# State-space layer: decay rows kept in DRAM in 4 copies, each read by 32 partitions, in place of 16 copies read by 8

## The chip, the core and the metric

The kernel runs on one core of one Trainium2 chip. The metric is the device time of one execution in microseconds; the time before is the median of 3 runs. A profiled execution of the same kernel gives the trace that all lines below come from; times in the trace count from the start of its span.

A core has a matmul engine (TensorE, PE in the profile, with its weight loads as PEld), a vector engine (VectorE, DVE), an engine for functions such as exp (ScalarE, ACT), a general engine (GpSimd, POOL) and an engine that here only issues DMA transfers (SyncE, SP). Sixteen DMA engines carry the transfers. Each engine runs its own instructions in a fixed order and waits on semaphores for the others. SBUF is the on-chip memory with 128 partitions, PSUM the accumulator of TensorE, DRAM the memory behind the DMA engines.

## The reference

The model is a trunk of two layers over 512 tokens of width 1024. Each layer is a feed-forward half step, a mixer and a second feed-forward half step, each with a layer norm. The mixer of the first layer is a bidirectional state-space layer with 32 heads of width 64, 4 groups of B and C, state size 128; that of the second layer is attention. What matters here, cut down:

```python
dt = softplus(dt_raw.reshape(b, t, 2, SSM_HEADS) + dt_bias)
A  = -exp(a_log)
# per direction, per head, in chunks:
a_cs         = cumsum(dt * A)
L            = exp(segsum(a))              # exp(a_cs[l] - a_cs[s]), masked to s <= l
CB           = einsum('bclgn,bcsgn->bgcls', Cc, Bc)
y_diag       = einsum('bgcls,bgjcls,bcsgjp->bclgjp', CB, L, Xc)
states       = einsum('bclgn,bgjcl,bclgjp->bcgjpn', Bc, exp(a_cs[-1] - a_cs), Xc)
y_off        = einsum('bclgn,bcgjpn,bgjcl->bclgjp', Cc, states, exp(a_cs))
y            = y_diag + y_off              # forward, and the same on the flipped sequence
y            = (y_f + y_b + X * d_skip) * silu(z)   # then a grouped RMS norm and a projection
```

So each head needs a decay matrix exp(a_cs[l] - a_cs[s] + log dt[s]) of tokens by tokens for each direction, and a row exp(a_cs[l]).

## The kernel before

Everything is kept transposed: features on the partitions, the 512 tokens along the free dimension. Weights come in units of 128 x 1024 floats (`load`, L99, one 512 KB transfer into one of four `raw` buffers), are split into a rounded high part (ScalarE, L123) and a low part (VectorE, L124), and each product is three matmuls (`mm3`, L166).

The function `ssm` (L589) is the state-space layer. `dt_proj` and `dt_chain` compute the cumulated decays with small matmuls and turn them so that heads lie on partitions and tokens along the free dimension: `rows` holds 32 heads of forward and 32 of backward decays, `rowe` the exponentials of them that go with the states. `dt_chain` ends with four transfers (L667) that write these rows to a DRAM tile `scr` (L602) of shape copies x 32 heads x 3 rows x 512 tokens. The write repeats each row once for every copy; its outer dimension is the 32 heads.

`ssd_head` (L757) is called for each of the 32 heads. It loads two rows of the head, spread over all 128 partitions, into the tile `rw` (L761, 512 KB, two buffers) and the third into `ch` (L763, 256 KB, three buffers), so that every partition (a source token s) holds the row over the destination tokens l. The source pattern is copies x (partitions per copy, step 0) x contiguous floats; rw reads 4 KB per partition, ch 2 KB. `ssd_head` then multiplies `ch` with C (VectorE, L764) and masks triangles of `rw` into `rw` and `dx` with GpSimd (L778).

`ssd_mats` (L783) builds for a head and a half (c = 0 or 1) of the tokens the matrix E: four exponentials on ScalarE (L786 to L789) with the source token's term as bias, a sum on GpSimd (L792) and a product with C·B on VectorE (L793). E has five buffers. `ssd_out` (L796) multiplies E, the states and `ch` into the PSUM tile `py`, whose pool tag is "mid" (L803); two heads share one `py`, so heads go in pairs, 16 pairs in all. After the second half of a pair VectorE adds the result into `xs` (L874).

The heads are dealt with in four groups of eight (`for g in range(NG)`). Between the steps of a group stand weight units as filler for TensorE: the next group's B, C and x projections, this group's z projections, and the output projection of the group before (`todo`, L863, L881). The layer ends with the norm of the last group and its output projection.

The order in which each engine runs its instructions is planned when the kernel is built, from the dependences, the order of the program text and estimated times; buffers of a pool are handed out in turn, and a transfer into a buffer waits until the last reader of its previous contents is done. All loads and the `scr` transfers are issued by SyncE in one queue.

Of the kernel before, what the change touches and what calls it, by code (L numbers as in the profile page):

```python
# [9 lines left out]
F32 = mybir.dt.float32  # L10
# [4 lines left out]
P = 128  # L15
T = 512
# [4 lines left out]
NA = 32  # L21
NE = 5
NG = 4
NST = 128
ALPHA = 4.0 ** 0.25
EPS = 1e-5
# [20 lines left out]
def hybrid_trunk(tc, xT, cb, par, cst, adaw, wgu, wdn0, wdn1, wdn2, wdt, win, wso, wqk, wv, wao, dist_in, dtp, lam_in, out):  # L47
    nc = tc.nc
# [13 lines left out]
    def big(dt=F32, name="big"):  # L62
        return ap.tile([P, T], dt, tag="a", name=name)

    def tmp(name="tmp"):
        return tp.tile([P, T], F32, tag="t", name=name)

    def acc(tag="acc"):
        return ps.tile([P, T], F32, tag=tag, name=tag, bufs=BANKS[tag])
# [519 lines left out]
    def ssm(n):  # L589
# [3 lines left out]
        dp = sc.enter_context(tc.tile_pool(name="dp", bufs=1, space=bass.MemoryType.DRAM))  # L593
# [5 lines left out]
        W = 256  # L599
        bias = ep.tile([P, 4, 64], F32, name="ssbias", bufs=1)  # L600
        dd = ep.tile([P, 4, 32], F32, name="dd", bufs=1)
        scr = dp.tile([16, 32, 3, T], F32, name="scr")  # L602

        def dt_proj():
            w = split(load(wdt, 512))
            pd = acc("mid")
            wk = [(w.hi[:, k * 64 : (k + 1) * 64], w.lo[:, k * 64 : (k + 1) * 64]) for k in range(KT)]
            proj(pd, wk, u, m=64, cols=HALVES)
            return pd

        def dt_chain(pd):
            dtT = tmp("dtT")
            nc.scalar.activation(dtT[:64], pd[:64], AF.Copy)
            pt = acc("ln")
            for i in range(4):
                nc.tensor.transpose(pt[:, i * 64 : (i + 1) * 64], dtT[:64, i * P : (i + 1) * P], ident[:64, :64])
            e1, e2, e3 = (ep.tile([P, T], F32, tag="E", name="E", bufs=NE) for _ in range(3))
            v, q, e, uu, lu = e1[:, :W], e1[:, W:], e2[:, :W], e2[:, W:], e3[:, :W]
            nc.vector.tensor_tensor(out=v, in0=pt[:, :W], in1=dtc[:, :W], op=ALU.add)
            nc.vector.scalar_tensor_tensor(out=q, in0=v, scalar=-1.0, in1=v, op0=ALU.mult, op1=ALU.max)  # L620
            nc.scalar.activation(e, q, AF.Exp, scale=-1.0)
            ea = e3[:, W:]
            nc.scalar.activation(ea, dtc[:, W:], AF.Exp)
            nc.vector.tensor_scalar(out=v, in0=v, scalar1=0.0, scalar2=None, op0=ALU.max)
            nc.vector.tensor_scalar(out=uu, in0=e, scalar1=1.0, scalar2=None, op0=ALU.add)
            nc.scalar.activation(lu, uu, AF.Ln)
            nc.vector.tensor_scalar(out=uu, in0=uu, scalar1=1.0, scalar2=None, op0=ALU.subtract)
            nc.vector.tensor_tensor(out=uu, in0=e, in1=uu, op=ALU.subtract)
            nc.vector.tensor_scalar(out=e, in0=e, scalar1=-0.5, scalar2=1.0, op0=ALU.mult, op1=ALU.add)
            nc.vector.tensor_tensor(out=uu, in0=uu, in1=e, op=ALU.mult)  # L630
            nc.vector.tensor_tensor(out=lu, in0=lu, in1=uu, op=ALU.add)
            nc.vector.tensor_tensor(out=v, in0=v, in1=lu, op=ALU.add)
            at = q
            nc.vector.scalar_tensor_tensor(out=at, in0=v, scalar=-1.0, in1=ea, op0=ALU.mult, op1=ALU.mult)
            nc.vector.tensor_scalar(out=v, in0=v, scalar1=1e-37, scalar2=None, op0=ALU.max)
            nc.scalar.activation(lu, v, AF.Ln)
            pcs = acc("ln")
            nones = tmp("nones")[:, :P]
            nc.gpsimd.memset(nones, -1.0)
            plan = {  # L640
                (0, 0): [(sgt, 0), (nones, 1)], (0, 1): [(sgt, 1)],
                (0, 2): [(sle, 2)], (0, 3): [(ones, 2), (sle, 3)],
                (1, 0): [(sge, 0), (ones, 1)], (1, 1): [(sge, 1)],
                (1, 2): [(slt, 2)], (1, 3): [(nones, 2), (slt, 3)],
            }
            for (dr, i), lst in plan.items():
                for k, (mk, j) in enumerate(lst):
                    nc.tensor.matmul(
                        pcs[:, i * 64 + dr * 32 : i * 64 + dr * 32 + 32], lhsT=mk,
                        rhs=at[:, j * 64 + dr * 32 : j * 64 + dr * 32 + 32],  # L650
                        start=k == 0, stop=k == len(lst) - 1,
                    )
            cs = tmp("cs")[:, :W]
            nc.scalar.activation(cs, pcs[:, :W], AF.Copy)
            nc.vector.tensor_tensor(out=bias.rearrange("p i h -> p (i h)"), in0=lu, in1=cs, op=ALU.subtract)
            pr = acc("ln")
            for i in range(4):
                nc.tensor.transpose(pr[:64, i * P : (i + 1) * P], cs[:, i * 64 : (i + 1) * 64], ident)
            rows = big(name="rows")
            nc.scalar.activation(rows[:64], pr[:64], AF.Copy)  # L660
            rowe = big(name="rowe")
            nc.scalar.activation(rowe[32:64, :W], pr[32:64, :W], AF.Exp)
            nc.scalar.activation(rowe[0:32, W:], pr[0:32, W:], AF.Exp)
            nc.scalar.activation(dd[:, 0:2, :], bias[:, 0:2, 0:32], AF.Exp)
            nc.scalar.activation(dd[:, 2:4, :], bias[:, 2:4, 32:64], AF.Exp)
            for j, a, b, src in ((0, 0, T, rows[0:32]), (1, 0, T, rows[32:64]), (2, 0, W, rowe[32:64]), (2, W, T, rowe[0:32])):
                nc.sync.dma_start(  # L667
                    scr[:, :, j, a:b].rearrange("r h x -> h r x"), src[:, a:b].unsqueeze(1).broadcast_to([32, 16, b - a])
                )

        last_in, last_exp = [None], [None]
# [24 lines left out]
        def units_bc(g, dst, cols=FULL, pre=None):  # L696
            def mk(e):
                return lambda: dst.append(conv(pre[e] if pre else split(load(win[g * 10 + e])), 16 + 4 * e + g, cols))
            return [mk(e) for e in range(2)]
# [57 lines left out]
        def ssd_head(h, Ct):  # L757

            src = scr[:, h].unsqueeze(1)
            rw = ep.tile([P, 2, T], F32, tag="rw", name="rw")  # L760
            nc.sync.dma_start(rw, src[:, :, 0:2].broadcast_to([16, 8, 2, T]))  # L761
            ch = ep.tile([P, T], F32, tag="ch", name="ch", bufs=3)
            nc.sync.dma_start(ch, src[:, :, 2].broadcast_to([16, 8, T]))  # L763
            nc.vector.tensor_tensor(out=ch, in0=ch, in1=Ct, op=ALU.mult)  # L764
            dx = ep.tile([P, 2, 2, P], F32, tag="dx", name="dx")
            f4 = rw[:, 0, :].rearrange("p (c o q) -> p c o q", c=2, o=2)
            b4 = rw[:, 1, :].rearrange("p (c o q) -> p c o q", c=2, o=2)
            for o, i_, fwd in (
                (f4[:, :, 0, :], f4[:, :, 0, :], True), (b4[:, :, 1, :], b4[:, :, 1, :], False),
            ):  # L770
                mask(o, i_, fwd)
            for o in range(2):
                mask(dx[:, :, o, :], (b4 if o == 0 else f4)[:, :, o, :], o == 1, inplace=False)
            return rw, ch, dx

        def mask(o, i_, fwd, inplace=True):
            sg = 1 if fwd else -1
            nc.gpsimd.affine_select(  # L778
                out=o, in_=i_, pattern=[[0, 2], [sg, P]], compare_op=ALU.is_ge,
                fill=-1.0e30, base=0, channel_multiplier=-sg,  # L780
            )
# [52 lines left out]
        def run(units):  # L834
            for f in units:
                f()

        pre = first_units(n)
        pd = dt_proj()
        bc, xs, zs = [], [], [[] for _ in range(NG)]  # L840
        run(units_bc(0, bc, cols=HALVES, pre=pre))
# [14 lines left out]

        for g in range(NG):
            xt, cbs, states, Ct = cur
            nbc, nxs = [], []
            first = units_z(g, zs[g])[len(zs[g]) :]  # L860
            if g < NG - 1:
                first = units_bc(g + 1, nbc) + units_x(g + 1, nxs) + first
            todo = first + ([lambda gg=g - 1: outp(gg)] * 4 if g > 0 else [])  # L863
            tot, done, batched = len(todo), 0, False
            for s in range(8):
# [13 lines left out]
                if s == 2 and norm is not None:  # L879
                    yrs[g - 1] = rest()  # L880
                while done < tot - (2 if g == NG - 1 else 0) and done < (s + 1) * tot // 8:  # L881
                    todo[done]()
                    done += 1
                if done >= len(first) and not batched and (s >= 6 or done == tot):
                    batched = True
                    silu(zs[g] + nbc + nxs)
                    if g < NG - 1:
                        cur = prepare(g + 1, nxs, nbc)
# [3 lines left out]
        run(todo[done:])  # L892
        for _ in down_units(n, yr, wide_units(wso[NG - 1]), True, 6):
            pass
# [168 lines left out]
    for d in range(KT):  # L1063
# [9 lines left out]
        for o in (hl[0], uf):  # L1073
            x = nc.scalar.activation(o, res[d], AF.Identity, bias=shift[0][:, d : d + 1], scale=onep[0][:, d : d + 1])
# [122 lines left out]
```

## Time and profile before

| | |
|---|---|
| median of 3 runs | 2179.48 us (2178.3 to 2181.34) |
| profiled execution, its own time | 2176.88 us |
| span of its trace | 2174.8 us |
| mean granted TensorE clock | 0.993 |
| busy share of the span: PE, PEld, DVE, ACT, POOL | 97%, 86%, 82%, 50%, 7% |
| DMA: bytes, mean rate | 301.18 MB, 138 GB/s |
| written to DRAM | 5.24 MB |
| first and last issue of an `rw` load | 429.0 us, 745.6 us |
| writes of `scr`: first and last issue | 416.9 us, 420.0 us |

How to read the lines. A row of a timeline has the start in us, the length in us, the engine, the line of the program, the operation, the tile written and the tiles read, their sizes, and a count; a bracket at the end gives idle time of the engine just before and what ended it. "SPq" rows are issues of transfers. A row of waits has who waited and for whom, us in all, times, and the longest. A row of a queue has packets, MB and the share of the time of all 16 DMA engines that the packets took. Shares of busy time are averages over stages that have different limits.

### The profile page before, as it was taken

What the parts mean: (1) busy time and instruction counts of PE and PEld (TensorE: products, weight loads), DVE (VectorE), ACT (ScalarE), POOL (GpSimd) and SP (SyncE); (2) the same over time, 40 slices, a digit from 0 to 9 for tenths busy, and PEclk for the clock granted to TensorE, in tenths of its full rate; (3) what the DMA queues carried; (4) which work ended last, traced back from release to release, by engine and by line L of the source; (5) the groups of instructions that cost most, each with busy time, mean ns of one, the idle gap of its engine ahead of it and who ended that gap; (6) DMA issues with size and microseconds to landing.
All of it is one profiled execution on the core that took longest, in us unless ns stands there. A gap on an engine that the chain in (4) does not pass through costs nothing.

```text
span 2174.8 us, 34198 instructions
## 1 busy us (share of the span) xinstructions
PE 2119.9 (97%) x13206; PEld 1859.7 (86%) x13206; DVE 1775.3 (82%) x3086; ACT 1092.4 (50%) x1828; POOL 154.2 (7%) x258
## 2 busy tenths in 40 slices
PE   7999999999999989999999999999999989999997
PEld 6889899866777778999999989899888869989897
DVE  6979899556766689989889998987877879858697
ACT  4424354767655546434356534343866637424353
POOL 0000000045232300000000000000111100000000
PEclk9999999999999999999999999999999989999999
DMA  9863644464535423646443273723322212323231
GB/s 324 302 212 121 219 138 149 123 183 137 158 123 155 121 68 126 214 144 198 159 132 105 97 261 96 254 94 111 98 80 79 76 59 78 127 69 117 84 110 39
DMA packets 90082, 301.18 MB, mean 138 GB/s; under 512 B 10048, under 2 KB 13504, under 8 KB 89920
## 3 DMA queue, kind: packets, MB, share of 16 engines
q1 hardware_dynamic: 88384, 294.81, 41.7%
q0 software_dynamic: 1536, 4.20, 0.9%
q8 instruction: 103, 1.69, 0.3%
q14 instruction: 59, 0.48, 0.1%
HBM read 289.53 MB, written 5.24 MB: 136 GB/s over the span
## 4 chain that ended last, share of the span: by engine, by line
PE 59%; DVE 3%; issue 2%; ACT 2%; POOL 1%; DMA 0%; POOLq 0%; ACTq 0%; DVEq 0%; SPq 0%
PE acc L166 47%; PE mid L166 9%; PE mid L965 1%; PE ln L166 1%; PE ln L987 0%; DVE resid L278 0%; DMA raw<-in_wgu 0%; DVE resid L320 0%; PE ln L253 0%; PE ln L302 0%; ACT p L975 0%; POOL E L792 0%; ACT wh L123 0%; PE ln L1004 0%; DVE p L968 0%
## 5 line engine op out<-in xcount | busy, mean ns | idle before, releaser
L166 PE MATMUL acc<-hi,wh 128*128 128x256 f32 (+1 forms) x1592 | 533.1, 336 | 9.2 <-DVE resid L372 7.1
L166 PE MATMUL acc<-hi,wl 128*128 128x256 f32 (+1 forms) x1592 | 532.6, 335 | 0.0
L166 PE MATMUL acc<-lo,wh 128*128 128x256 f32 (+1 forms) x1592 | 532.1, 335 | 0.1
L166 PE MATMUL acc<-uh,wh 128*128 128x256 f32 (+1 forms) x1160 | 391.2, 338 | 0.0
L166 PE MATMUL acc<-ul,wh 128*128 128x256 f32 (+1 forms) x1160 | 389.6, 336 | 0.0
L166 PE MATMUL acc<-uh,wl 128*128 128x256 f32 (+1 forms) x1160 | 388.9, 336 | 0.0
L123 ACT ACTIVATE wh<-raw 128x1024 fp32r<-128x1024 f32 (+1 forms) x210 | 212.8, 1021 | 277.5 <-PE acc L166 95.4
L166 PEld LDWEIGHTS acc<-hi,wh 128*128 128x128 f32 x1592 | 302.9, 190 | 45.5 <-DVE resid L372 6.6
L470 ACT ACTIVATE wh<-raw 128x1024 fp32r<-128x1024 f32 x198 | 209.1, 1059 | 259.4 <-DVE raw L480 129.1
L166 PEld LDWEIGHTS acc<-lo,wh 128*128 128x128 f32 x1592 | 302.9, 190 | 31.0 <-DVE lo L154 1.3
L166 PEld LDWEIGHTS acc<-hi,wl 128*128 128x128 f32 x1592 | 303.0, 190 | 30.3 <-issue 0.5
L124 DVE TENSOR_TENSOR wl<-raw,wh 128x1024 fp32r<-128x1024 f32 (+1 forms) x210 | 248.4, 1185 | 46.7 <-ACT wh L123 45.4
L471 DVE TENSOR_TENSOR wl<-raw,wh 128x1024 fp32r<-128x1024 f32 x198 | 240.8, 1219 | 38.9 <-ACT wh L470 38.1
L166 PEld LDWEIGHTS acc<-uh,wh 128*128 128x128 f32 x1160 | 219.0, 189 | 28.6 <-issue 6.2
L166 PEld LDWEIGHTS acc<-ul,wh 128*128 128x128 f32 x1160 | 219.3, 189 | 25.1 <-issue 3.2
L166 PEld LDWEIGHTS acc<-uh,wl 128*128 128x128 f32 x1160 | 219.2, 189 | 23.7 <-issue 2.4
L480 DVE TENSOR_TENSOR raw<-raw 128x512 f32<-128x512 f32 x264 | 181.3, 688 | 5.0
L184 DVE SCALAR_TENSOR_TENSOR raw<-raw,cond 128x1024 f32<-128x1024 f32 x144 | 174.1, 1218 | 9.9 <-DMA raw<-in_adaw 9.7
L372 DVE SCALAR_TENSOR_TENSOR resid<-acc,gv,resid 128x512 f32<-128x512 f32 (+1 forms) x166 | 109.4, 663 | 58.8 <-PE acc L166 58.4
L316 POOL TENSOR_TENSOR rr<-vr,mhalf 128x2 f32<-128x2 f32 x12 | 8.4, 698 | 1527.6 <-DVE vr L312 1527.6
L166 PE MATMUL mid<-uh,wh 128*128 128x256 f32 (+2 forms) x332 | 99.8, 302 | 0.0
L166 PE MATMUL mid<-uh,wl 128*128 128x256 f32 (+2 forms) x332 | 99.3, 299 | 0.0
(266 smaller groups left out, 3920.7 us busy)
## 6 DMA issues: line engine op xcount, KB each, us to landing
raw<-in_wgu SPq DMA_DIRECT2D x176, 512.0 KB, 4.2
raw<-in_adaw SPq DMA_DIRECT2D x144, 512.0 KB, 4.6
raw<-in_wdn SPq DMA_DIRECT2D x64, 448.0 KB, 4.0
raw<-in_win SPq DMA_DIRECT2D x40, 512.0 KB, 4.2
raw<-in_wdn SPq DMA_DIRECT2D x32, 512.0 KB, 4.4
rw<-scr SPq DMA_DIRECT2D x32, 512.0 KB, 5.5
ch<-scr SPq DMA_DIRECT2D x32, 256.0 KB, 3.6
raw<-in_wso SPq DMA_DIRECT2D x16, 512.0 KB, 3.5
```

The source lines that it names most:

```text
L123: nc.scalar.activation(hi[:, :n], raw, AF.Copy)
L124: nc.vector.tensor_tensor(out=lo[:, :n], in0=raw, in1=hi[:, :n].bitcast(F32), op=ALU.subtract)
L166: last = nc.tensor.matmul(o, lhsT=a, rhs=b, start=start and j == 0, stop=j == n - 1, skip_group_check=not start)
L184: nc.vector.scalar_tensor_tensor(out=raw, in0=raw, scalar=1.0, in1=cond, op0=ALU.mult, op1=ALU.mult, accum_out=mods[l][:, j : j + 1],)
L316: nc.gpsimd.tensor_tensor(out=r[:, :m], in0=vr[:, :m], in1=mhalf[:, :m], op=ALU.pow)
L372: nc.vector.scalar_tensor_tensor(out=res[d][:, a:b], in0=pd[:, a:b], scalar=gvec[n][:, d : d + 1], in1=res[d][:, a:b], op0=ALU.mult, op1=A ...
L470: nc.scalar.activation(x[0], r, AF.Copy)
L471: nc.vector.tensor_tensor(out=x[1], in0=r, in1=x[0].bitcast(F32), op=ALU.subtract)
L480: nc.vector.tensor_tensor(out=o, in0=x, in1=y, op=ALU.add)
L965: nc.tensor.matmul(ss[m], lhsT=q[:, c], rhs=qks[h, 1][m], start=j == 0, stop=j == 1)
```

## The change

The number of copies becomes a constant NREP = 4. The DRAM tile `scr` gets 4 copies instead of 16, the four writes repeat each row 4 times instead of 16, and each of the 64 loads of `rw` and `ch` reads 4 copies, each by 32 partitions, instead of 16 copies by 8. The number of transfers, the bytes each load brings into SBUF and all computation stay as they are.

```diff
+NREP = 4
...
-        scr = dp.tile([16, 32, 3, T], F32, name="scr")
+        scr = dp.tile([NREP, 32, 3, T], F32, name="scr")
...
                 nc.sync.dma_start(
-                    scr[:, :, j, a:b].rearrange("r h x -> h r x"), src[:, a:b].unsqueeze(1).broadcast_to([32, 16, b - a])
+                    scr[:, :, j, a:b].rearrange("r h x -> h r x"), src[:, a:b].unsqueeze(1).broadcast_to([32, NREP, b - a])
                 )
...
-            nc.sync.dma_start(rw, src[:, :, 0:2].broadcast_to([16, 8, 2, T]))
+            nc.sync.dma_start(rw, src[:, :, 0:2].broadcast_to([NREP, P // NREP, 2, T]))
             ch = ep.tile([P, T], F32, tag="ch", name="ch", bufs=3)
-            nc.sync.dma_start(ch, src[:, :, 2].broadcast_to([16, 8, T]))
+            nc.sync.dma_start(ch, src[:, :, 2].broadcast_to([NREP, P // NREP, T]))
```

## The prediction

> **What bounds the kernel now.** I read the page, then busy time by stretch of the state-space stage, then waits, then the order of time. The page:
>
> ```profile
> DMA packets 90082, 301.18 MB, mean 138 GB/s; under 512 B 10048, under 2 KB 13504, under 8 KB 89920
> q1 hardware_dynamic: 88384, 294.81, 41.7%
> ```
>
> The DMA engines are 42% used over the span, so they do not bound it as a whole. The 10,048 packets under 512 B are 628 transfers with 16 each: every transfer of this kernel was spread over all 16 engines. The heads of the stage run from about 429 to 771 us; busy time by stretch (PE, PEld, DVE, ACT, POOL; clock; DMA share):
>
> ```profile
> 429.00:530.00 101.00, 95.45 (x432) 64.63 (x432) 57.66 (x75) 67.86 (x146) 43.39 (x71) 0.98 0.64 172
> 720.00:771.00 51.00, 48.31 (x245) 35.15 (x243) 34.71 (x49) 27.39 (x54) 17.52 (x27) 1.00 0.47 136
> ```
>
> Columns are the stretch, its length, then busy time of each engine. TensorE is the bound (95.45 of 101, 48.31 of 51), but it is idle for 5.6 us at the front and 2.7 us at the back, so something else ends last there. Who waits there (engine and line, what for, us in all, times, longest; the first from 429 to 771 us, the other two from 410 to 771 us):
>
> ```profile
> POOL rw L778 <- DMA rw<-scr: 153.1, 29, 51.6
> SPq L761 <- ACT E L787: 47.1, 20, 9.9
> SPq L761 <- DMA scr<-rows: 6.5, 2, 5.3
> ```
>
> POOL waits for the landing of rw in 29 places. Only two rw buffers exist, so the next pair's load is issued when ACT has read this pair's. Load, mask (POOL), exponentials (ACT), sum (POOL), product (DVE), matmul "mid" is therefore a loop; what lengthens the load lengthens it.
>
> **The change part by part.** Bytes read and the number of loads stay: 32 rw and 32 ch. What each costs an engine now comes from the transfers of 429 to 767 us, one raw load alone (613.2 to 618.5 us), one ch load alone (757.2 to 763.0 us), and the rate in 40 slices of 719.97 to 726.5 us (an rw load):
>
> ```profile
> rw<-scr SPq DMA_DIRECT2D x32, 512.0 KB, 5.5
> raw<-in_win SPq DMA_DIRECT2D x28, 512.0 KB, 4.8
> ch<-scr SPq DMA_DIRECT2D x32, 256.0 KB, 3.6
> raw<-in_wso SPq DMA_DIRECT2D x16, 512.0 KB, 3.5
> ...
> q1 hardware_dynamic: 144, 0.52, 30.0%
> raw<-in_win SPq DMA_DIRECT2D x1, 512.0 KB, 3.4
> ...
> q1 hardware_dynamic: 144, 0.26, 15.1%
> ...
> GB/s 0 0 251 100 25 50 376 401 427 401 427 427 301 50 100 276 100 125 226 401 351 427 226 326 226 151 100 75 75 0 0 0 0 0 0 0 0 0 0 0
> ```
>
> A load is 128 rows, 8 on each of 16 engines (144 packets are 128 + 16). Raw: 0.300 x 5.3 us x 16 / 128 = 0.199 us per 4 KB row, 1.59 us per engine; it lands 3.4 us after issue, so 1.8 us are fixed (1.3 ahead, 0.5 behind, my split). ch: 0.151 x 5.8 x 16 / 128 = 0.109 us per 2 KB row. At the peak, 427 / 16 = 26.7 GB/s, a row takes 0.153 or 0.077 us; the rest is a start of about 0.36 or 0.27 us per load.
>
> The Trainium skill (DMA: Bandwidth & Descriptors, Specifications) gives about 27 GiB/s per engine, 29 GB/s, which would make a 4 KB row 0.141 us by estimate, 8% less than the peak here; the row decides.
>
> *Reads.* Sixteen copies read by eight is one copy per engine. The source pattern's leading count falls from 16 to 4, and if the spread follows it, four engines carry each load, 32 rows each. Every transfer of this trace leads with a multiple of 16, so no row shows a narrower spread; I take it because 16 copies on 16 engines is what that split looks like, and 32 rows then cost rw 32 x 0.153 + 0.36 = 5.3 us (6.4 at 0.199) and ch 32 x 0.077 + 0.27 = 2.7 us (3.5 at 0.109). If all 16 still share, both ends fall to today's 1.6 and 0.9.
>
> The Trainium skill (DMA: Bandwidth & Descriptors, "Why a DMA increments its semaphore by 16 and not by 1") says that a transfer uses the largest number of engines up to 16 that divides the slowest dimension of both patterns, here 4 of 4 and 128. No run here shows it yet; by that rule the four-engine sum below holds, without it the 16-engine rival.
>
> On those four engines the stretch 429 to 767 us would hold 32 x (5.3 + 2.7) + 44 x 1.59 = 326 us of work in 338 us (387 us at the upper ends), against some 150 us now. They become a nearly full queue in order, and raws wait behind. Raws have four buffers, so they can land late; rw cannot. The front, by issues (SP), masks of a pair's second head (POOL) and "mid" (PE):
>
> ```profile
> 461.09 1.16 SPq L763 DMA_DIRECT2D ch<-scr  x2
> 462.30 1.92 SPq L99 DMA_DIRECT2D raw<-in_win  x3
> 464.38 1.79 SPq L761 DMA_DIRECT2D rw<-scr  x2
> 469.55 0.33 SPq L99 DMA_DIRECT2D raw<-in_win  x1
> 473.68 1.16 SPq L763 DMA_DIRECT2D ch<-scr  x2
> 474.94 0.53 SPq L99 DMA_DIRECT2D raw<-in_win  x1
> 480.70 1.61 SPq L761 DMA_DIRECT2D rw<-scr  x2
> ...
> 477.24 0.77 POOL L778 TENSOR_SCALAR_AFFINE_SELECT rw<-rw 128x256 f32<-128x256 f32 x2 [0.21 <-DMA rw<-scr]
> 487.75 0.76 POOL L778 TENSOR_SCALAR_AFFINE_SELECT rw<-rw 128x256 f32<-128x256 f32 x2 [0.22 <-DMA rw<-scr]
> 500.93 0.77 POOL L778 TENSOR_SCALAR_AFFINE_SELECT rw<-rw 128x256 f32<-128x256 f32 x2
> ...
> 480.79 1.08 PE L803 MATMUL mid<-E,xt 128*64 128x256 f32 x2 [3.56 <-DVE E L793]
> 494.33 0.62 PE L803 MATMUL mid<-E,xt 128*64 128x256 f32 x2 [0.72 <-DVE E L793]
> 515.66 0.65 PE L803 MATMUL mid<-E,xt 128*64 128x256 f32 x4
> ```
>
> With the engines free at 462.4: two ch (5.4), three raws (4.8), two rw (10.6) end at 483.2; landing 483.7, mask 6.5 us later than 477.24. TensorE waits at that "mid" already (3.56), so 6.5 us are lost, and the next pair's issue moves to 487.2. Raw, two ch, raw (8.6), then two rw end at 502.4; landing 502.9, 15.2 us later than 487.75, at a "mid" again without slack (0.72). The following pair has 14.7 us from mask 500.93 to "mid" 515.66 where the two before had 3.6 and 6.6; its own lateness of about 19 us fits into that and the 15 already lost. Front: +15. Bounds: if ch and raws do not stand ahead of rw, the first pair lands at 464.4 + 1.8 + 10.6 = 476.8, on time, and the next at 493.1, +5; at the upper row times (two rw 12.8, two ch 7.0) three rounds come 3 us later each, +24. Behind the waiting masks on POOL stand the sums (L792) of the heads before; behind the waiting exponentials on ACT stand the weight splits (L123) that feed TensorE.
>
> In the middle the same lateness meets a long cover:
>
> ```profile
> 604.85 0.92 POOL L778 TENSOR_SCALAR_AFFINE_SELECT rw<-rw 128x256 f32<-128x256 f32 x2 [3.26 <-DMA rw<-scr]
> 636.92 1.08 PE L803 MATMUL mid<-E,xt 128*64 128x256 f32 x8
> ```
>
> This pair's second mask is 32 us ahead of its "mid", so an rw that lands 10 to 15 us later is hidden there, and I price it at 0. If the cover is gone because ACT holds its splits back, it is the lateness over what three split weight units give TensorE in advance; that goes into the upper end.
>
> The tail, where the last head decides:
>
> ```profile
> 726.63 1.16 SPq L763 DMA_DIRECT2D ch<-scr  x2
> 729.27 0.51 SPq L761 DMA_DIRECT2D rw<-scr  x1
> 738.39 0.52 SPq L761 DMA_DIRECT2D rw<-scr  x1
> 741.28 1.17 SPq L763 DMA_DIRECT2D ch<-scr  x2
> 745.65 0.51 SPq L761 DMA_DIRECT2D rw<-scr  x1
> ...
> 734.62 1.01 POOL L778 TENSOR_SCALAR_AFFINE_SELECT rw<-rw 128x256 f32<-128x256 f32 x2 [3.27 <-DMA rw<-scr]
> 743.16 0.83 POOL L778 TENSOR_SCALAR_AFFINE_SELECT rw<-rw 128x256 f32<-128x256 f32 x2 [4.02 <-DMA rw<-scr]
> 750.57 0.76 POOL L778 TENSOR_SCALAR_AFFINE_SELECT rw<-rw 128x256 f32<-128x256 f32 x2 [2.86 <-DMA rw<-scr]
> ...
> 771.60 1.05 PE L817 MATMUL ln<-invg,gss 128*128 128x1 f32 x8 [2.22 <-DVE gss L814]
> ```
>
> Each of these masks ends a POOL wait for its load. Two ch from 727.9 to 733.3, rw to 738.6, landing 739.1: +4.5. The next issue moves to 742.9, its load ends at 749.5, landing 750.0: +6.8. Two ch, then the last rw, ends at 760.2, landing 760.7: +10. TensorE waits at 771.60 for what follows, so the tail costs +10. Bounds: +2 if only the last load's own time counts (7.1 us against 750.57 - 745.65 = 4.9), +14 at the upper row times.
>
> *Writes.* Four instructions stay, moving a quarter. rw waits 6.5 us for them now. TensorE's cover:
>
> ```profile
> 416.80:429.00 12.20, 12.20 (x58) 10.12 (x57) 6.65 (x8) 9.53 (x16) 0.00 (x0) 1.00 0.91 181
> ```
>
> TensorE is full (12.20 of 12.20) while they hold the DMA engines at 0.91, so the shorter wait is worth 0. At most it is worth the 5.6 us of idle time at the front, if the head start were carried along; a loss is excluded, since fewer bytes go through the same four instructions. Where that cover is gone, it costs nothing either, as a shorter wait makes nothing late.
>
> Sum: 15 + 10 + 0 = +25. The profiled execution took 2176.9 us (span 2174.8), 2.6 below the median of 2179.5, so the predicted median is 2176.9 + 25 + 2.6 = 2204.5, **2204** us.
>
> **The rivals.** *Sixteen engines remain.* Reads cost what they do; the writes' quarter brings rw forward, worth 0 to 5.6 us: 2174 to 2179.5. For it: all 628 transfers use 16. Against it: none led with 4. It decides if the small packets stay 10,048. This is the side of faster. *Four engines, hidden.* If masks came early by the head start (about 7 us) and the order of issue let ch and raws fall behind rw, the front's +5 and the tail's +2 shrink to under 4 us: 2180 to 2183. Against it: TensorE already waits at two front "mid"s. *Four engines, saturated.* At 387 us of work in 338 us the stage stretches by 49: 2228. For it: rows under load are slower than 0.153. A further unknown is the order of instructions, which is planned at build time from estimates and may move; I give it 4 us either way.
>
> **How the numbers follow.** Four engines with a loop that lengthens 0.67; saturated 0.13; hidden 0.09; sixteen 0.11. Slower by over 0.2% (4.4 us, about what a measurement of this kernel tells from no change): 0.82, the first two and a little of hidden. Within: 0.12. Faster: 0.06, half of sixteen. Range for 8 in 10: from 2182 (front +5 and tail +2, less the order's 4) to 2230 (saturated); the likeliest case alone spans 2186 to 2220.
>
> **What would show it.** Small packets 9,280 (10,048 less 64 x 12) if the other engines send none; rw landing in 7 us alone, 10 to 20 in the queue, instead of 5.5, ch over 4.5; POOL's wait for rw well over 153 us in all; TensorE idle at "mid" in 460 to 530 us grown by about 15 us; the last mask to TensorE's norm matmul unchanged but later; scr written in under 5 us. After the stage nothing moves. The prediction is wrong if rw lands in 5.5 us as before, or if it lands late and TensorE's idle time in 429 to 771 us stays near 8 us.

## The result and the profile after

| | before | after |
|---|---|---|
| median | 2180.03 us (4 runs, 2178.3 to 2181.34) | 2302.91 us (4 runs, 2301.94 to 2305.12) |
| ratio to before | 1 | 1.0565, 95% interval 1.0552 to 1.0579 |
| profiled execution (span) | 2176.88 us (2174.8) | 2303.0 us (2300.1) |
| mean granted clock | 0.993 | 0.971 |

The change makes the kernel 123 us slower. The forecast was +25 us, with 2230 as the top of its range: the direction was right, the size was missed by a factor of five.

From the page of the kernel after (busy times, packets, the queue that carries the loads):

```profile
PE 2149.9 (93%) x13206; PEld 1874.1 (81%) x13206; DVE 1771.2 (77%) x3086; ACT 1091.1 (47%) x1828; POOL 137.7 (6%) x258
DMA packets 87779, 298.82 MB, mean 130 GB/s; under 512 B 9280, under 2 KB 11968, under 8 KB 87616
q1 hardware_dynamic: 86080, 292.45, 38.2%
```

Small packets fell by 768, which is 64 x 12: each of the 64 loads of rw and ch now uses 4 engines in place of 16. The Trainium skill says that an outermost dimension of c copies, with c below 16, keeps a DMA to at most c engines (page "DMA: Bandwidth & Descriptors", section "Rules for kernel authors"); the traces agree, with 9,280 for 4 copies here and 9,536 (10,048 less 64 x 8) for 8 copies below. The queue takes a smaller share than before (38.2% against 41.7%). The first row of the page of the kernel before was:

```profile
PE 2119.9 (97%) x13206; PEld 1859.7 (86%) x13206; DVE 1775.3 (82%) x3086; ACT 1092.4 (50%) x1828; POOL 154.2 (7%) x258
```

PE executes the same 13,206 matmuls and is busy 30.0 us longer (2149.9 against 2119.9). The remaining 95 of the 125.3 us that the span grew are idle time of PE.

Where it sits, in the busy time by stretch of the kernel after (stretch, length, PE, PEld, DVE, ACT, POOL, granted clock, DMA share, GB/s):

```profile
430.00:530.00 100.00, 67.63 (x288) 44.92 (x288) 37.82 (x51) 41.90 (x93) 28.64 (x53) 0.85 0.36 117
530.00:630.00 100.00, 77.62 (x353) 54.72 (x352) 46.61 (x66) 47.63 (x96) 20.92 (x41) 0.90 0.29 92
630.00:730.00 100.00, 84.78 (x367) 62.21 (x368) 47.73 (x63) 47.11 (x92) 20.30 (x39) 0.91 0.32 103
730.00:830.00 100.00, 78.60 (x332) 55.77 (x331) 50.63 (x68) 45.47 (x88) 16.46 (x34) 0.88 0.33 103
```

Not the front alone, but every 100 us of the stage of heads leave PE idle for 15 to 32 us. No engine is full in them, and the DMA engines are on average less busy than before (0.29 to 0.36, against 0.64 in the prediction's row from 429 us): everything waits for something late. What for, in the waits of the kernel after from 425 to 900 us (engine and line, what for; us in all, times, longest):

```profile
POOL rw L779 <- DMA rw<-scr: 235.1, 31, 10.7
ACT dx L789 <- POOL dx L779: 127.0, 16, 10.6
ACT E L787 <- POOL rw L779: 68.4, 15, 9.5
DVE wl L125 <- ACT wh L124: 59.3, 20, 8.6
PE mid L804 <- DVE ch L765: 45.6, 9, 10.5
DVE ch L765 <- DMA ch<-scr: 41.3, 13, 7.5
```

The same view of the kernel before has for the second and third:

```profile
ACT dx L788 <- POOL dx L778: 36.1, 13, 4.5
ACT E L786 <- POOL rw L778: 17.7, 5, 6.3
```

POOL's wait for rw grew from 153.1 to 235.1 us, and it now reaches ScalarE: ACT stands idle 195.4 us (127.0 + 68.4) ahead of the exponentials of a head, against 53.8. The weight loads are not what is late: no row of the same view has ACT waiting for a `raw` load. The split of a weight unit is late all the same, since DVE waits 59.3 us for ACT's part of it (L124; 21.9 us before). PE's own waits in that view are 45.6 us for the product with ch (L765), 34.4 for what ACT alone makes (SiLU L714, copies L724 and L745), 17.4 for xd, which DVE makes from one of these copies (L748), and only 3.0 for the product E of DVE (L794), at the end of the loop that the prediction walked. How a late rw gets to all these places is what the experiments show.

One turn of the loop, from the timeline of the kernel after (start, duration, queue or engine and line, operation; in brackets the idle time before it and what ended it):

```profile
486.67 0.53 SPq L762 DMA_DIRECT2D rw<-scr  x1
487.25 1.15 SPq L764 DMA_DIRECT2D ch<-scr  x2
489.68 1.33 SPq L762 DMA_DIRECT2D rw<-scr  x1
...
495.66 0.76 POOL L779 TENSOR_SCALAR_AFFINE_SELECT rw<-rw 128x256 f32<-128x256 f32 x2 [5.26 <-DMA rw<-scr]
506.99 0.76 POOL L779 TENSOR_SCALAR_AFFINE_SELECT rw<-rw 128x256 f32<-128x256 f32 x2 [8.60 <-DMA rw<-scr]
...
498.89 0.69 DVE L765 TENSOR_TENSOR ch<-ch,xc 128x512 f32<-128x512 f32 x1 [6.50 <-DMA ch<-scr]
...
499.63 1.11 PE L804 MATMUL mid<-ch,st 128*64 128x256 f32 x2 [10.54 <-DVE ch L765]
```

The first rw reaches its mask 9.0 us after its issue, the first ch its product 11.6, the second rw its mask 17.3 (506.99 - 489.68): the loads stand in line on their four engines. TensorE waits 10.54 us for ch here, a wait that the prediction did not walk.

### The profile page after: what moved, and what is told of

Its sections match the earlier page's. It is cut to its first block, busy times and chain, and to the rows that moved or that the text cites. A ratio compares the mean times of both kernels' runs of the same rounds, so it can differ in the third digit from the quotient of the medians.

```text
span 2300.1 us, 34196 instructions
## 1 busy us (share of the span) xinstructions
PE 2149.9 (93%) x13206; PEld 1874.1 (81%) x13206; DVE 1771.2 (77%) x3086; ACT 1091.1 (47%) x1828; POOL 137.7 (6%) x258
## 2 busy tenths in 40 slices
DMA packets 87779, 298.82 MB, mean 130 GB/s; under 512 B 9280, under 2 KB 11968, under 8 KB 87616
## 3 DMA queue, kind: packets, MB, share of 16 engines
q1 hardware_dynamic: 86080, 292.45, 38.2%
## 4 chain that ended last, share of the span: by engine, by line
PE 55%; DVE 4%; issue 4%; ACT 2%; POOL 1%; DMA 1%; POOLq 0%; ACTq 0%; DVEq 0%; SPq 0%
PE acc L167 43%; PE mid L167 8%; PE mid L966 1%; PE ln L167 1%; DMA raw<-in_wgu 1%; PE ln L988 0%; POOL E L793 0%; DVE resid L279 0%; PE ln L254 0%; DVE resid L321 0%; DVE wl L125 0%; DVE lo L155 0%; PE ln L303 0%; ACT wh L124 0%; PE ln L1005 0%
## 5 line engine op out<-in xcount | busy, mean ns | idle before, releaser
L124 ACT ACTIVATE wh<-raw 128x1024 fp32r<-128x1024 f32 (+1 forms) x210 | 212.5, 1020 | 253.3 <-DMA raw<-in_wdn 97.3
L472 DVE TENSOR_TENSOR wl<-raw,wh 128x1024 fp32r<-128x1024 f32 x198 | 240.9, 1220 | 39.2 <-ACT wh L471 38.1
L794 DVE TENSOR_TENSOR E<-E,cb 128x512 f32<-128x512 f32 x64 | 45.7, 724 | 73.9 <-POOL E L793 69.2
```

Of the source, the lines that this page charges most:

```text
L124: nc.scalar.activation(hi[:, :n], raw, AF.Copy)
L472: nc.vector.tensor_tensor(out=x[1], in0=r, in1=x[0].bitcast(F32), op=ALU.subtract)
L794: nc.vector.tensor_tensor(out=E, in0=E, in1=cbs[c], op=ALU.mult)
```

## The experiments

Each edit is told against the kernel after. Intervals are 95%, each against the kernel before on the same chip. The kernel before took 2179.1 to 2181.0 us in each of these series, so that the medians can be compared. "ACT idle" is the sum of the two rows above (ACT for POOL's dx and for POOL's rw, 425 to 900 us); where a view has no such row, it counts as nothing.

| run | copies written / read, what leads | runs | median us | ratio | small packets | ACT idle us |
|---|---|---|---|---|---|---|
| before | 16 / 16, 16 copies | 4 | 2180.0 | 1 | 10,048 | 53.8 |
| after | 4 / 4, 4 copies | 4 | 2302.9 | 1.0565 | 9,280 | 195.4 |
| lead32 | 4 / 4, 32 repeats | 6 | 2172.56 | 0.9965 [0.9951, 0.9979] | 10,048 | 38.8 |
| write16_read4 | 16 / 4, 4 copies | 4 | 2287.12 | 1.0487 [1.0468, 1.0507] | 9,280 | 179.1 |
| lead4_32copies | 32 / 32, 4 repeats | 2 | 2314.43 | 1.0616 [1.0591, 1.0641] | 9,280 | 193.4 |
| rw4_ch16 | 4 / 4, rw 4, ch 32 | 4 | 2274.74 | 1.0428 [1.0406, 1.045] | 9,664 | 164.3 |
| rw16_ch4 | 4 / 4, rw 32, ch 4 | 4 | 2221.77 | 1.0189 [1.0175, 1.0203] | 9,664 | 112.9 |
| copies8 | 8 / 8, 8 copies | 4 | 2223.68 | 1.0196 [1.0182, 1.021] | 9,536 | 107.4 |
| bufs | 4 / 4, 4 copies, a buffer more | 2 | 2241.18 | 1.0277 [1.0258, 1.0296] | 9,280 | 107.0 |
| one | 1 / 1, 128 partitions | 9 | 2174.82 | 0.9971 [0.9962, 0.9981] | 10,049 | 38.1 |
| rw_twice | 4 / 4, 32 repeats, rw loaded twice | 4 | 2201.59 | 1.0102 [1.0086, 1.0118] | 10,560 | 80.1 |
| write16_lead32 | 16 / 4, 32 repeats | 7 | 2172.37 | 0.9963 [0.9952, 0.9975] | 10,048 | 40.5 |
| bufs_lead32 | 4 / 4, 32 repeats, a buffer more | 2 | 2169.12 | 0.995 [0.9932, 0.9969] | 10,048 | 33.0 |

**Four copies, sixteen engines (lead32).** The same four copies are read, each by 32 partitions, but the repeat is the outermost dimension and the copy the second. Its instructions stand in exactly the order of the kernel after, on every engine.

```
-  nc.sync.dma_start(rw, src[:, :, 0:2].broadcast_to([NREP, P // NREP, 2, T]))
+  nc.sync.dma_start(rw, scr[:, h].unsqueeze(0)[:, :, 0:2].broadcast_to([P // NREP, NREP, 2, T]))
-  nc.sync.dma_start(ch, src[:, :, 2].broadcast_to([NREP, P // NREP, T]))
+  nc.sync.dma_start(ch, scr[:, h].unsqueeze(0)[:, :, 2].broadcast_to([P // NREP, NREP, T]))
```

> Still 4 copies, each read by 32 partitions, and the instruction order of the changed kernel on every engine; only the loads' pattern is turned: 32 repeats outermost, copies inside, so the leading count is 32. Theory (the leading count sets how many DMA engines carry a load): 16 engines again, 10,048 small packets, rw lands in about 5.5 us, time 2174 to 2184, the whole +123 us gone. Rival (32 partitions reading one copy is what is slow): stays at 2290 to 2305 with long 4 KB packets. Rival (the instruction order that the smaller writes brought is what is slow): stays near 2303 with rw landing in 5.5 us.

Measured: 2172.56 us. The whole loss is gone, and 7 us below the kernel before. From its page (issue, count, KB, us to landing), then its waits from 425 to 900 us:

```profile
rw<-scr SPq DMA_DIRECT2D x32, 512.0 KB, 4.6
```

```profile
POOL rw L779 <- DMA rw<-scr: 119.2, 28, 41.6
ACT dx L789 <- POOL dx L779: 30.4, 18, 3.5
...
ACT E L787 <- POOL rw L779: 8.4, 5, 2.8
```

With 10,048 small packets the load lands after 4.6 us (5.5 before), and ACT's idle time falls to 38.8 us. So, with sixteen engines, neither the smaller writes nor the 32 readers of a copy nor this order of instructions costs anything; what leads the read does.

**The old order and the old writes (write16_read4).** All 16 copies are written as before, and four of them are read with the copy outermost. Its instructions stand in exactly the order of the kernel before.

```
-  scr = dp.tile([NREP, 32, 3, T], F32, name="scr")
+  scr = dp.tile([16, 32, 3, T], F32, name="scr")
   ...
-  ... src[:, a:b].unsqueeze(1).broadcast_to([32, NREP, b - a])
+  ... src[:, a:b].unsqueeze(1).broadcast_to([32, 16, b - a])
   ...
-  src = scr[:, h].unsqueeze(1)
+  src = scr[0:NREP, h].unsqueeze(1)
```

> All 16 copies are written as in the kernel before, and the instruction order of every engine is that of the kernel before; the loads read only 4 of the copies, 32 partitions each, leading count 4. Theory (engines): about 2300 (2285 to 2315), 9,280 small packets. Rival (order of instructions): about 2180. Rival (sharing of a copy): about 2300 too, so this run only tells the order apart.

Measured: 2287.12 us, so 107 of the 123 us come with the reads alone. Because nothing moved, each instruction can be laid beside its counterpart of before. Busy time by stretch, first of the kernel before, then of this one, cut at the same instructions as nearly as whole us allow:

```profile
429.00:500.00 71.00, 66.28 (x302) 43.73 (x301) 40.78 (x53) 40.13 (x89) 28.73 (x50) 0.98 0.71 188
500.00:711.00 211.00, 207.36 (x991) 153.01 (x990) 140.38 (x187) 138.02 (x273) 71.66 (x118) 1.00 0.46 138
711.00:772.00 61.00, 57.71 (x295) 42.14 (x294) 42.23 (x59) 32.87 (x64) 18.29 (x28) 1.00 0.44 129
```

```profile
429.00:524.00 95.00, 69.49 (x296) 45.48 (x294) 40.98 (x54) 41.74 (x88) 26.41 (x48) 0.87 0.45 137
524.00:802.00 278.00, 231.63 (x1003) 165.11 (x1002) 138.10 (x187) 136.90 (x273) 62.90 (x119) 0.91 0.34 106
802.00:882.00 80.00, 63.98 (x296) 45.24 (x297) 42.63 (x60) 32.83 (x64) 15.88 (x28) 0.89 0.31 99
```

The front grew by 24 us, the middle by 67, the tail by 19; together 110, as much as the span (2285.4 less 2174.8). Of the middle's 67 us, 43 are idle time of PE (46.4 against 3.6) and 24 are PE's longer busy time for nearly the same work (1003 matmuls against 991) at a granted clock of 0.91 in place of 1.00. The Trainium skill has the clock halved after an idle window of about 3.4 us until the engine has been busy for as long (page "TensorE: Matmul & The Clock Gate", Part 1); the traces agree in the main. In the kernel after the clock is halved for 3.4 to 17.1 us at a time, 105.8 us of the stretch from 425 to 900 us, against 10.2 in the kernel before, and the longest of these begins in PE's longest gap (15.89 us, until 559.23). But PE need not have been idle all the time: in the 3.4 us ahead of such a stretch it was busy for up to 1.4.

How a late load takes time from the middle can be followed at the very pair at which the prediction found 32 us of cover (mask 604.85, "mid" 636.92). Its counterpart in the timeline of write16_read4, with what ACT and PE did a little earlier:

```profile
635.69 0.40 ACT L789 ACTIVATE dx<-dx,ssbias 128x128 f32<-128x128 f32 x1 [8.48 <-POOL dx L779]
636.95 1.04 ACT L124 ACTIVATE wh<-raw 128x1024 fp32r<-128x1024 f32 x1
...
641.40 3.22 ACT L714 ACTIVATE xc<-xc 128x512 f32<-128x512 f32 x6
...
649.43 0.57 ACT L724 ACTIVATE bt<-ln 128x512 f32<-128x512 f32 x1
...
650.06 2.07 PE L730 MATMUL ln<-xc 128*128 128x256 f32 x4 [5.76 <-ACT bt L724]
...
669.98 0.77 POOL L779 TENSOR_SCALAR_AFFINE_SELECT rw<-rw 128x256 f32<-128x256 f32 x2 [8.78 <-DMA rw<-scr]
671.14 0.40 ACT L789 ACTIVATE dx<-dx,ssbias 128x128 f32<-128x128 f32 x1 [4.33 <-POOL dx L779]
...
672.38 0.57 ACT L745 ACTIVATE xt<-ln 128x512 f32<-128x512 f32 x1
672.99 0.69 DVE L748 TENSOR_TENSOR xd<-xt,dd 128x512 f32<-128x512 f32 x1 [4.81 <-ACT xt L745]
673.74 1.12 PE L752 MATMUL ln<-xd,bt 128*128 128x512 f32 x2 [2.33 <-DVE xd L748]
...
700.41 1.08 PE L804 MATMUL mid<-E,xt 128*64 128x256 f32 x8
```

From mask to "mid" there are still 30.4 us (32.1 before): the cover at "mid" was real, and no time is lost there. It is lost on the way. ACT works in order; at 671.14 it has stood 4.33 us for this pair's masked block, and the copy xt behind it (L745), which does not need the load at all, comes only at 672.38. DVE waits 4.81 us for that copy, and PE 2.33 us for DVE, 27 us ahead of the "mid" that was looked at. The rows above show the same with the pair before: ACT's 8.48 us hold back a weight split (L124), the SiLU (L714) and the copy bt (L724), and PE then waits 5.76 us for bt.

These are not two chosen places. What PE waits for in the whole middle of write16_read4 (524 to 802 us) is, in the longest rows:

```profile
PE ln L730 <- ACT bt L724: 11.0, 2, 5.8
PE mid L804 <- DVE ch L765: 10.5, 3, 6.9
PE ln L722 <- ACT xc L714: 7.0, 3, 3.6
PE ln L752 <- DVE xd L748: 6.6, 5, 2.3
PE ln L743 <- ACT xt L745: 4.6, 2, 2.5
```

In the same stretch before (500 to 711 us), PE waits 3.4 us for xd and 0.2 for xt, and for none of the others. So 29.2 us end with bt, xc, xd or xt, none of which needs the load, and only 3.6 us with E at "mid". The 10.5 us for ch are of the same kind, by DVE's order. The longest of them:

```profile
753.72 0.69 DVE L794 TENSOR_TENSOR E<-E,cb 128x512 f32<-128x512 f32 x1 [8.42 <-POOL E L793]
754.33 1.21 DVE L765 TENSOR_TENSOR ch<-ch,xc 128x512 f32<-128x512 f32 x1
...
755.60 1.12 PE L804 MATMUL mid<-ch,st 128*64 128x256 f32 x2 [6.90 <-DVE ch L765]
```

DVE has stood 8.42 us for POOL's sum of a head with a late rw; the product with ch stands behind it and starts without a wait of its own. Followed back along ACT and DVE, each of these waits that is over 0.3 us (39.7 us in all with the shorter ones) comes from a place where ACT stands for POOL's masks or DVE for POOL's sum.

**Only one of the two loads on four engines (rw4_ch16, rw16_ch4).** From the kernel after, the line of the other load is replaced as in lead32. Both keep the order of the kernel after.

```
rw4_ch16:
-  nc.sync.dma_start(ch, src[:, :, 2].broadcast_to([NREP, P // NREP, T]))
+  nc.sync.dma_start(ch, scr[:, h].unsqueeze(0)[:, :, 2].broadcast_to([P // NREP, NREP, T]))
rw16_ch4:
-  nc.sync.dma_start(rw, src[:, :, 0:2].broadcast_to([NREP, P // NREP, 2, T]))
+  nc.sync.dma_start(rw, scr[:, h].unsqueeze(0)[:, :, 0:2].broadcast_to([P // NREP, NREP, 2, T]))
```

> As the changed kernel, but the 32 ch loads have 32 repeats outermost; only the rw loads keep a leading count of 4. Theory (engines, and the ch load waiting behind rw is the larger part, since TensorE waits about 95 us at mid for the product with ch): the ch waits go, 2210 to 2250, 9,664 small packets. Rival (the rw loop through GpSimd and ScalarE carries the loss): 2270 to 2300.

> As the changed kernel and in its order, but the rw loads have 32 repeats outermost; only the ch loads keep a leading count of 4, so 9,664 small packets. Four engines carry about 16 x 2 x 2.7 = 87 us of ch work in the stage. Theory (what costs is that rw lands late, since ScalarE runs in order and holds the weight splits behind its exponentials; ch alone is small): 2172 to 2195, against 2172.6 with both on 16 engines and 2274.7 with only rw on 4. Rival (ch late is as bad by itself, since TensorE waits for its product in the changed kernel): 2210 or more.

Measured: 2274.74 and 2221.77 us, 102 and 49 above lead32, where the two together cost 130. Both expectations of mine missed. In the first I had given ch the larger part, after the 10.54 us at one "mid"; its rival (the rw loop, through POOL and ACT) is right. In the second I had given ch alone next to nothing; its rival has the size (2210 or more), but not the way: PE waits only 11.1 us for the product with ch there (45.6 in the kernel after), while ACT's idle time is 112.9 us. So ch alone acts largely through rw. In rw16_ch4, where rw itself uses 16 engines, POOL waits from 425 to 900 us:

```profile
POOL rw L779 <- DMA rw<-scr: 170.7, 28, 40.0
```

That is 51.5 us more than in lead32, and the trace shows why. It has 16 updates of a load's semaphore, and four of them come late where ch rows are queued ahead: for the rw load issued at 729.7 us, right behind two ch loads, twelve come by 7.0 us after the issue and the last four at 9.0 to 10.9. In 12 of the 32 rw loads the thirteenth update is over 1 us behind the twelfth; in lead32 and in the kernel before that happens in none.

**Other counts of copies (lead4_32copies, copies8, one).** lead4_32copies writes 32 copies and reads each by 4 partitions, with the 4 repeats outermost, so that only the leading 4 is kept of the change; its instructions stand in the order of the kernel before. copies8 and one change the constant alone, and their order was partly replanned.

```
lead4_32copies:
-  NREP = 4
+  NREP = 32
   and both loads as in lead32 (outermost P // NREP = 4)
copies8:  NREP = 8        one:  NREP = 1
```

> 32 copies are written, and each is read by 4 partitions only, but the loads repeat 4 times outermost, so the leading count is 4. Theory (engines): as slow as the changed kernel or a little slower, as twice the bytes are written: 2295 to 2330, 9,280 small packets. Rival (sharing of a copy by many readers): faster than the kernel before had no reason to be slow, about 2180 to 2200, as no copy has more readers than before.

> 8 copies, each read by 16 partitions, leading count 8. Theory: 8 engines per load, 9,536 small packets (10,048 less 64 x 8), rw 16 x 0.153 + 0.36 = 2.8 us and ch 1.5 us on each of the 8: the pair's four loads take 8.6 us instead of 16, so the lateness of a pair's second rw falls from 6 to 12 us to 1 to 4; if cost follows lateness beyond what TensorE has in advance, 2178 to 2205. Rival (cost proportional to the rows per engine beyond 8, a third of the changed kernel's excess): 2172 + 130 x 8/24 = 2215.

> One copy only, read by all 128 partitions, leading count 128 (a single copy has no dimension of its own). Theory (engines by the leading count): 16 engines, 10,048 small packets, as fast as the kernel with 4 copies and 32 repeats outermost, 2168 to 2178, so faster than both the kernel before and the changed one. Rival (readers of one copy collide): slower than that kernel, 2185 or more.

Measured: 2314.43, 2223.68 and 2174.82 us. With few readers of many copies, four engines are as bad as with many readers of few; with one copy read by all 128 partitions sixteen engines are as good as lead32. So many readers of one address cost nothing that can be seen here. Eight engines cost 44 us above before: my 2178 to 2205 missed, as it again took most of the lateness to be covered; the rival that made the cost proportional to the rows per engine (2215) was nearer.

**Is it the loop? (bufs).** The kernel after with one more buffer for rw and for ch. The instructions were replanned with it.

```
-  rw = ep.tile([P, 2, T], F32, tag="rw", name="rw")
+  rw = ep.tile([P, 2, T], F32, tag="rw", name="rw", bufs=3)
-  ch = ep.tile([P, T], F32, tag="ch", name="ch", bufs=3)
+  ch = ep.tile([P, T], F32, tag="ch", name="ch", bufs=4)
```

> The changed kernel with a third rw buffer and a fourth ch buffer, leading count 4, so the loads can be issued earlier; the order of instructions is planned anew and differs in many places. Theory (a loop of latency: the four engines are busy only some 320 of 465 us, and two buffers let a pair's load start only when ScalarE has read the last pair's): a good part comes back, 2220 to 2270. Rival (the four engines are saturated): 2295 to 2310.

Measured: 2241.18 us, 62 less than after, with the same 9,280 packets on the same four engines. Four engines that are full would not go faster with more room; so they were not full, and about half of the loss over lead32 (62 of 130) is the latency of a load that is issued only when a buffer comes free. SyncE's own waits agree: from 425 to 900 us it stands 129.8 us ahead of rw loads until ACT has read the old contents in the kernel after, 46.8 us here and 45.0 in lead32. A part of the 62 may belong to the other order of instructions; with sixteen engines that order is worth nothing that can be told (bufs_lead32, below), but with four it was not tried apart.

**Lateness without four engines (rw_twice).** lead32, with each rw load issued twice in a row into the same buffer; the mask waits for the second. The order of instructions was partly replanned.

```
+  nc.sync.dma_start(rw, scr[:, h].unsqueeze(0)[:, :, 0:2].broadcast_to([P // NREP, NREP, 2, T]))
   (a second time, behind the first)
```

> The kernel with 4 copies and 32 repeats outermost (16 engines, 2172.6), but every rw load is issued twice into the same buffer, the second after the first has landed; nothing else is left out or changed. No load is on four engines, the rw tile is only complete some 4 to 5 us later. Theory (a late rw costs, by whatever means, because ScalarE stands at its exponentials): ScalarE's idle time before the exponentials rises from 39 us to about 90 to 130 and the time to 2205 to 2250, as with 8 copies. Rival (four overloaded engines as such, through the late weight units or the full queue, are what costs): 2172 to 2190.

Measured: 2201.59 us, 29 above lead32, between the two expectations and nearer to the theory's 2205. Its waits from 425 to 900 us:

```profile
ACT E L787 <- POOL rw L779: 50.5, 18, 7.9
ACT dx L789 <- POOL dx L779: 29.6, 9, 7.3
```

With all 16 engines in use the late block makes ACT idle for 80.1 us (38.8 in lead32; 90 to 130 were expected) and the kernel slower. So a late rw costs without four engines, too. Not all else is equal: SyncE stands 97.2 us for the first of the two loads, so that later loads are issued later (DVE's wait for ch is 17.8 us, 4.5 in lead32), and the order differs in places. Over the runs time goes nearly with ACT's idle time, which ties the two but does not by itself make one the cause of the other: a straight line through lead32 and after, 2172.6 + 0.83 x (ACT idle - 38.8), gives 2277 for rw4_ch16 (2274.7 measured), 2289 for write16_read4 (2287.1), 2230 for copies8 (2223.7), 2234 for rw16_ch4 (2221.8), 2207 for rw_twice (2201.6), 2229 for bufs (2241.2) and 2301 for lead4_32copies (2314.4, the farthest off).

**Where lead32's gain is from, and the best version (write16_lead32, bufs_lead32).** write16_lead32 has the writes and the exact order of before, and reads four copies with the 32 repeats outermost; bufs_lead32 is lead32 with the buffers of bufs, in the same order of instructions as bufs.

```
write16_lead32: scr and its writes as in write16_read4, and
+  nc.sync.dma_start(rw, scr[0:NREP, h].unsqueeze(0)[:, :, 0:2].broadcast_to([P // NREP, NREP, 2, T]))
   (ch likewise)
bufs_lead32: lead32 with bufs=3 for rw and bufs=4 for ch
```

> 16 copies written and the instruction order of the kernel before on every engine; the loads read 4 of the copies with 32 repeats outermost, so 16 engines. It differs from the kernel before only in which copies the loads read. If the gain of 4 copies and 16 engines (2172.6) came from the smaller writes or the order that they brought: 2176 to 2183, no change. If it came from reading fewer copies: 2168 to 2175.

> A third rw and a fourth ch buffer as in the run with leading count 4 (2241.2), in exactly that run's order, but with 32 repeats outermost, so 16 engines. It gives what that order is worth by itself. Theory: the order is not what lost the rest, 2165 to 2180, so the leading count of 4 still costs 60 to 75 us there against 130 with two buffers. Rival: the replanned order is itself bad, 2200 or more.

Measured: 2172.37 and 2169.12 us. The first equals lead32 (2172.56): the gain of 7 to 8 us over before is one of the reading pattern, not of the writes or the order. From the page of write16_lead32:

```profile
rw<-scr SPq DMA_DIRECT2D x32, 512.0 KB, 4.8
```

Here as in lead32 the load lands 0.7 to 0.9 us sooner than the 5.5 of before, with as many packets on as many engines; why it does was not tried. bufs_lead32 (0.995 [0.9932, 0.9969]) is the fastest that was run and beats both kernels; from lead32 its two runs do not tell it apart. Beside bufs, which has its order, it says that four engines cost 72 us even with the third buffer.

## Why the prediction was right in kind and wrong in size

- *Four engines.* Right: 9,280 small packets, and lead32 takes the whole loss back by what leads the access pattern.
- *Landing of rw 10 to 20 us in the queue, ch over 4.5, writes in under 5.* Right, with rw at the low end: by the updates of their semaphores in the trace of the kernel after, the 32 rw loads land 7.9 to 17.9 us after their issue (median 10.1), the 32 ch loads 5.3 to 19.6 (median 9.9), the four writes in 2.7 to 3.9.
- *Writes, 0.* Right for sixteen engines: 16 copies written (write16_lead32) and 4 (lead32) take the same time.
- *The front, +15 (5 to 24).* Mis-sized: 24 us, the upper bound (by its own row times a round gets 3.8 us later, not 3, so that bound would be 26). In write16_read4 the two "mid"s of the walk come 18.1 and 24.3 us late, where it had 6.5 and 15.2:

```profile
498.84 1.08 PE L804 MATMUL mid<-E,xt 128*64 128x256 f32 x2 [8.07 <-DVE E L794]
...
518.62 1.09 PE L804 MATMUL mid<-E,xt 128*64 128x256 f32 x2 [6.73 <-DVE E L794]
```

What it adds was nearly right (5.8 us for the first of the two pairs, where it had 6.5); its start was not. The walk begins with the engines free at 462.4 and the pair's rw loads issued at 464.38, as before. But the heads from 430 us on already read over four engines, and in write16_read4 these two loads are issued only at 476.67, 12.3 us late:

```profile
476.67 1.89 SPq L762 DMA_DIRECT2D rw<-scr  x2
```

- *The tail, +10 (2 to 14).* Mis-sized: 19 us, 12.7 of it more idle time of PE (16.0 against 3.3) and 6.3 longer busy time. The place was another one as well: of the 16.0 us, 15.3 are waits for the product with ch, the longest of them (9.97) behind a product E for which DVE has stood 5.04 us; the norm matmul that the prediction looked at waits only 0.6.
- *The middle, 0.* This is the step that failed: "This pair's second mask is 32 us ahead of its 'mid', so an rw that lands 10 to 15 us later is hidden there". It costs 67 us. The cover was measured from the mask to the one matmul that uses its result. But ACT's queue, in order, has other work right behind the exponentials of that head (splits, SiLU, copies of turned tiles), and DVE's has the product with ch behind that with E; PE needs these within a few us. The cover that counts is that of the next instruction behind the waiting one on the same engine, and it was near nothing: 39.7 us of PE's waits there (29.2 and 10.5 above) come that way, and some 24 us are PE's longer busy time. The text named the condition itself ("because ACT holds its splits back") and put it into the upper end, but no term of the range holds it. The lateness also does not stop after three pairs: each next load waits for an ACT that is already late (SyncE's 129.8 us above), so every pair pays again.
- *The clock.* Not in the sum at all. In the stretches with idle gaps the granted clock is 0.85 to 0.91, and PE's busy time in the kernel after is 30.0 us longer, a quarter of the loss.
- *ch.* Its loads were put ahead of rw's in the queue, but not walked to PE, which waits 45.6 us for its product in the stage. Up to 530 us that is 19.0 us, with DVE waiting for the load of ch itself (10.54 above); later most of it is ch's product standing behind a late E. By itself on four engines ch costs 49 us over lead32.
- *Saturated, 2228.* Short of the time, and not the cause: bufs takes 62 us off with the same rows on the same engines.
- *Order of instructions, 4 us either way.* Nothing with 16 engines (lead32 against write16_lead32). But after and write16_read4 differ by 16 us, and only by the order and the size of the writes. Smaller writes are hardly the reason: with the same order as write16_read4 and twice its copies written, lead4_32copies (4 readers to a copy) issues its first rw load 10.2 us later and is 27 us slower. That leaves the order; the largest single difference seen is PE's wait for SiLU (L714) of 15.89 us at 559.23 in the kernel after, against 3.58 at 539.63 in write16_read4. How four engines make it matter stays open.

## What to carry to other kernels

Where a load is late, don't look only for the instruction that uses its result: find the engine that first waits for it, and price what stands behind that instruction in its queue. Put the zero-stride repeats of a broadcast outermost, in a count that is a multiple of 16 (32 and 128 were run), and the copies inside: the same bytes of the same four copies took 2172.56 us in one nesting and 2302.91 in the other. A loop with two buffers turns a longer load into waiting time at every turn; one more buffer, with the order that came with it, gave half of the loss back.

## What was not expected of the hardware

- A load kept to four engines also delays the loads that use all sixteen: with ch alone on four, POOL's wait for a sixteen-engine rw went from 119.2 to 170.7 us, and where the two were queued four of the 16 updates of rw's semaphore came up to 3.6 us behind the other twelve.
- Idle gaps of up to 15.9 us come with a lower clock, so that TensorE pays a second time: 13,206 matmuls in 2149.9 us against 2119.9.
- Readers of one copy seem not to matter: on sixteen engines 128 partitions per copy took 2174.82 us and 32 took 2172.56; on four engines 4 per copy were no faster than 32 (2314.43 against 2302.91).
